# Layer 0's scans: two channel tiles at once, as two chains half a step apart

## The chip, the cores and the metric

The kernel runs on one core of a Trainium2 chip. The metric is the device time of one execution in microseconds (us). All arithmetic is in float32; the large matmuls are made of products of operands split into a rounded upper part (`whi`) and a rest (`wlo`).

## What is computed

A backbone of two layers over 256 latent tokens and a prefix of 256 context tokens, model width 2048. Each layer: a norm, a modulation by the condition, a mixer, a gated residual add. Layer 0 is a bidirectional delta-rule recurrence (32 heads of 64), layer 1 a bidirectional retention. The change concerns the recurrence of layer 0, whose step is

```
def wkv7_scan(S0, r, decay, k, v, kk, a, reverse):
    def step(S, inp):
        r_t, w_t, k_t, v_t, kk_t, a_t = inp
        sa = jnp.einsum('bhvk,bhk->bhv', S, kk_t)
        S = S * w_t[:, :, None, :] - sa[..., None] * (kk_t * a_t)[:, :, None, :] + v_t[..., None] * k_t[:, :, None, :]
        return S, jnp.einsum('bhvk,bhk->bhv', S, r_t)
...
    for d in range(2):
        S_c, oc = wkv7_scan(S0, r_c, w_c[d], k_c[d], v_c, kk_c, a_c[d], d == 1)
        _, ol = wkv7_scan(S_c, r_l, w_l[d], k_l[d], v_l, kk_l, a_l[d], d == 1)
```

## The kernel before

Channels lie in 16 tiles of 128 (two heads each); a tile is called e. Layer 0 first projects (0 to about 500 us), then works out features for every tile (to about 1015 us) and stores them in device memory (`fD`, `vcD`, and triangular blocks whose inverses come back as `Td`, `T1d`), then runs the scans (about 1018 to 1748 us), then a tail (to 1800 us) before layer 1.

The recurrence is done in chunks of 64 tokens: 8 steps for a tile, each for both directions. A step has four links, each on the result of the one before: **z** (L1322, two matmuls with the states, then a DVE add with `zv`, L1327), **u** (L1340, two matmuls with the inverted blocks `tt`, then two ACT copies, L1346), the **state products** (L1353, two matmuls, called m in the prediction), and the **state updates** (four DVE operations, L1366, or L1368 in a tile's first step). The next z needs the updates. This is "the chain".

What a step needs beforehand is made for half a tile (4 steps, a "set"; argument `hf`): `loads` brings features (`ft`, L1210 and L1213) and values (`uv`, L1219) into one of FR = 4 buffers, `tloads` brings inverses (`tt`, L1247, and `t1`, L1242), and `ahead` computes `zv` (L1263), `first` (L1277) and `second` (L1294). Behind the 4 steps come the **outs** of the set (L1399 and L1406), which use the same buffers and then free them, so that the loads of the set two further on can start. `back` finishes a tile (norm, gate; L1450 and L1460 are its transposes), and `out_chunk` multiplies finished tiles with the output weights (L1524, 512 columns a matmul) in groups of GR tiles and adds the sums to `x1` (L1533).

The order of PE, DVE, ACT and POOL is fixed by a planner, the class `Wheel`: every piece of work is given with a planned time (`W.at`), pieces are written out by planned time as soon as their buffers are free in that order, and each of these engines runs its instructions in exactly that order. A matmul that waits therefore holds everything behind it on PE. The DMA issues on SyncE (SP) are left to the scheduler, which orders them by their place in the program and by priority. PSUM has one bank each for z (`ps_p`), u with the state products (`ps_u`) and the outs (`ps_o`), three for the output chunks (`ps_b0`, `ps_b1`, `ps_t`, by `BANK`) and two for the rest (`ps_c`). `ada_line` (L350) computes parts of the condition's modulation in the tail.

The planned pace of a tile is `TE`, 40 us for the first four and 34.5 for the others.

## Time and profile before

| | us |
|---|---|
| median of 3 runs | 2850.48 |
| lowest and highest run | 2847.07 and 2854.71 |
| the profiled execution | 2847.56 |
| its span in the trace | 2845.8 |
| PE busy in the span | 2695.4 (95%) |
| mean granted TensorE clock | 0.98 |

Rows of the profile that matter here are of four kinds. A *stretch* gives the busy time of each engine between two times, the granted TensorE clock (1.00 is full speed) and the share of time in which the DMA engines were busy. A *wait* gives the engine and line that waited, what released it, the sum, the count and the longest. A *group* gathers the instructions of one line and shape: busy time, mean ns of one, and the idle time of the engine just before them. A *timeline* row has a start, a duration, the line and a count of like instructions in a row; the bracket is idle time before it. Matmuls are pipelined, so the duration of a row overlaps the next; starts tell more. PE is the matmul, PEld its weight load.

### The profile page before, as it was taken

The page shows a single profiled execution, that of the slowest core. Times are in us where ns is not written, and L with a number is a line of the kernel's source. Part 1 is how long each engine was busy: PE and PEld are TensorE (multiplying, and loading weights), DVE is VectorE, ACT ScalarE, POOL GpSimd, SP SyncE. Part 2 cuts the span into 40 slices and gives each one's busy share as a digit, 9 for nine tenths or more (in the row PEclk, how much of TensorE's full clock was granted, in tenths as well). Part 3 has the DMA queues.
Part 4 walks back from the last instruction along what each step waited for, and adds up shares of the span by engine and source line. Part 5 has one row for each costly group of instructions (what it writes and reads, how often), then busy time and mean ns, then how long its engine had stood idle before and what let it go on. Part 6 is the DMA issues. An engine that isn't in the chain of part 4 may idle for free. (4 is left out here: it accounts for less than half of the span.)

```text
span 2845.8 us, 48362 instructions
## 1 busy us (share of the span) xinstructions
PE 2695.4 (95%) x18564; PEld 2132.3 (75%) x18580; DVE 1695.0 (60%) x3142; ACT 1330.1 (47%) x2284; POOL 494.4 (17%) x368
## 2 busy tenths in 40 slices
PE   6999999999998999989888899999999999999998
PEld 4576478777776777766666676788888898899886
DVE  3565843688888754567665635875555554434444
ACT  5243732577776434444443443545444543334443
POOL 0002300000013322222212222220000079800000
PEclk9999999999999999989999999999999999999999
DMA  9778974578887766565665555565545576644654
GB/s 339 286 254 299 317 238 127 157 222 267 265 271 245 249 171 192 177 218 169 183 184 153 162 164 197 181 225 175 185 166 177 206 251 226 221 138 150 206 183 163
DMA packets 490425, 594.73 MB, mean 209 GB/s; under 512 B 122689, under 2 KB 306897, under 8 KB 487377
## 3 DMA queue, kind: packets, MB, share of 16 engines
q1 hardware_dynamic: 490194, 591.64, 64.3%
q8 instruction: 146, 2.39, 0.3%
q14 instruction: 85, 0.70, 0.1%
HBM read 464.11 MB, written 127.40 MB: 208 GB/s over the span
## 5 line engine op out<-in xcount | busy, mean ns | idle before, releaser
L394 DVE TENSOR_TENSOR wlo<-wraw,whi 128x1024 fp32r<-128x1024 f32 (+1 forms) x368 | 461.0, 1254 | 567.6 <-ACT whi L393 559.9
L393 ACT CAST whi<-wraw 128x1024 fp32r<-128x1024 f32 (+1 forms) x368 | 375.7, 1024 | 601.2 <-PE ps_acc L420 177.8
L420 PE MATMUL ps_acc<-whi,xop 128*128 128x512 f32 x1024 | 304.9, 392 | 1.3 <-DVE ev L642 0.8
L1895 PE MATMUL ps_acc<-xop,whi 128*128 128x256 f32 (+1 forms) x1024 | 255.6, 342 | 3.6 <-ACT whi L393 2.4
L420 PEld LDWEIGHTS ps_acc<-whi,xop 128*128 128x128 f32 x1024 | 192.0, 188 | 45.3 <-issue 2.9
L1895 PEld LDWEIGHTS ps_acc<-xop,whi 128*128 128x128 f32 x1024 | 178.0, 192 | 27.0 <-ACT whi L393 2.8
L1795 PEld LDWEIGHTS ps_b<-ax,xop 128*128 128x128 f32 x1536 | 190.9, 189 | 4.9 <-DVE ah L394 0.3
L1795 PE MATMUL ps_b<-ax,xop 128*128 128x256 f32 x1536 | 194.5, 283 | 0.1
L1366 DVE SCALAR_TENSOR_TENSOR s<-ps_u,ec,qs 64x64 f32<-64x64 f32 x384 | 108.6, 283 | 134.6 <-PE ps_u L1353 123.1
L420 PE MATMUL ps_acc<-wlo,xop 128*128 128x512 f32 x512 | 187.4, 393 | 0.0
L726 PE MATMUL ps_acc<-xop,whi 128*128 128x512 f32 x512 | 177.5, 406 | 2.0 <-DVE ev L642 2.0
L577 PE MATMUL ps_acc<-xop,whi 128*128 128x512 f32 x512 | 161.8, 402 | 14.8 <-ACT xop L393 13.6
L1895 PE MATMUL ps_acc<-xop,wlo 128*128 128x256 f32 (+1 forms) x512 | 172.2, 338 | 0.0
L1845 PE MATMUL ps_acc<-whi,ah 128*128 128x512 f32 x512 | 161.5, 396 | 2.1 <-DVE ah L394 2.1
L420 PE MATMUL ps_c<-whi,xop 128*128 128x512 f32 x512 | 155.3, 391 | 0.0
L1515 POOL TENSOR_TENSOR wlo<-wraw,whi 128x512 fp32r<-128x512 f32 (+2 forms) x56 | 81.7, 1458 | 363.5 <-ACT whi L1514 313.7
L1524 PE MATMUL ps_b<-yx,whi 128*128 128x512 f32 x352 | 141.0, 447 | 3.8 <-DVE x L1533 3.8
L1868 POOL TENSOR_TENSOR wga<-wga,cst 128x512 f32<-128x512 f32 x64 | 70.1, 1116 | 417.0 <-DVE xop L394 404.9
L1346 ACT ACTIVATE uv<-ps_u 64x128 f32<-64x128 f32 x256 | 69.5, 271 | 149.8 <-PE ps_u L1340 147.5
L577 PEld LDWEIGHTS ps_acc<-xop,whi 128*128 128x128 f32 x512 | 96.0, 191 | 54.0 <-ACT xop L393 17.3
L771 POOL TENSOR_TENSOR wlo<-wraw,whi 128x1024 fp32r<-128x1024 f32 x32 | 78.4, 2451 | 211.8 <-ACT whi L770 207.0
L420 PEld LDWEIGHTS ps_acc<-wlo,xop 128*128 128x128 f32 x512 | 96.7, 189 | 20.8 <-issue 0.5
(303 smaller groups left out, 5731.3 us busy)
## 6 DMA issues: line engine op xcount, KB each, us to landing
wada<-in_ada_w SPq DMA_DIRECT2D x72, 1024.0 KB, 8.5
wraw<-in_rt_w_in SPq DMA_DIRECT2D x64, 1024.0 KB, 5.2
ft<-fD SPq DMA_DIRECT2D x64, 768.0 KB, 6.5
wraw<-in_rk_w_in SPq DMA_DIRECT2D x72, 512.0 KB, 4.6
fD<-it SPq DMA_DIRECT2D x64, 512.0 KB, 4.3
wraw<-in_rt_w_in SPq DMA_DIRECT2D x64, 512.0 KB, 4.8
wraw<-in_rt_w_out SPq DMA_DIRECT2D x32, 1024.0 KB, 5.2
wraw<-in_rk_w_in SPq DMA_DIRECT2D x28, 1024.0 KB, 5.6
```

Source lines behind the costliest of these rows:

```text
L393: self.nc.scalar.copy(hi, src)
L394: (eng or self.nc.vector).tensor_tensor(lo, src, hi.bitcast(F32), ALU.subtract)
L420: nc.tensor.matmul(pt, xop(d)[:, x_, xs], ws[k // 2][w_][:, k % 2, sl], start=(d == 0 and n == 0), stop=(d == nk - 1 and n == 2))
L577: nc.tensor.matmul(acc[i], (hi, lo)[w_][:, kk, 128 * i:128 * i + 128], xs[ds[k]][:, x_, :], start=(k == 0 and n == 0), stop=(k == nk - 1 a ...
L726: nc.tensor.matmul(st["acc"][i], st["s", d // 4][w_][:, d % 4, 128 * i:128 * i + 128], self.kx[d][:, x_, :], start=(d == 0 and m == 0), st ...
L771: nc.gpsimd.tensor_tensor(st["s", c][1], st["w", c], st["s", c][0].bitcast(F32), ALU.subtract)
L1366: nc.vector.scalar_tensor_tensor(dst, src, ec, R["qs", d][H, H], ALU.mult, ALU.add)
L1515: nc.gpsimd.tensor_tensor(lo[:, 0:n, :], src, hi[:, 0:n, :].bitcast(F32), ALU.subtract)
L1524: nc.tensor.matmul(Q["p", i], Q["s", i // 2][w_][:, k, 128 * (i % 2):128 * (i % 2) + 128], st["yx", e0 + k][:, x_, :], start=(k == 0 and r ...
L1795: nc.tensor.matmul(pt[:, TL * j:TL * j + TL], ht[e][:, w_, 128 * k:128 * k + 128], ax[:, k, x_, :], start=(k == 0 and n == 0), stop=(k == ...
L1845: nc.tensor.matmul(acc[m], y[:, x_, kk, 128 * m:128 * m + 128], ws[w_][:, kk, :], start=(p == 0 and kk == 0 and n == 0), stop=(p == 7 and ...
L1895: nc.tensor.matmul(acc[i][:, 0:nt], w_[:, kk, 128 * i:128 * i + 128], x[:, x_, 0:nt], start=(d == 0 and n == 0), stop=(d == KD - 1 and n = ...
```

## The change

The tiles are taken in pairs E, E+1. Each tile of a pair is a chain of its own, and the second is half a step behind the first. Sets are quarters now (`q`, two steps of both tiles), with eight feature buffers of half the size. Each chain has one PSUM bank (`ps_p0`, `ps_p1`) in which z, u and both state products lie side by side, and each tile of a pair has a bank for its outs; the output chunks have two banks. The feature array `fD` is laid out in quarters, so its stores are runs of half the length. `back` of the odd tile comes BO = 21 us after that of the even one, the output groups are [2, 4, 4, 2, 2, 2] tiles, and the ada lines come in eight pieces of half the size. Line numbers move: `zv` is L1272, `first` L1284, `second` L1297, z L1327, u L1346, the state products L1359, the outs L1408 and L1415, the output matmuls L1540, the loads L1215, L1216 and L1221, `tt` L1253 and `t1` L1250, the transposes of `back` L1461 and L1471.

In the middle of the scans PE had, of the kernel before, the links of one chain with output matmuls between them (names: output<-moving and stationary operand):

```order
L1353 MATMUL ps_u<-uv,ft_8746 128x128
L1353 MATMUL ps_u<-uv,ft_8748 128x128
L1524 MATMUL ps_b_13420<-yx,whi 128x512
L1450 MATMUL ps_c<-c_ident,vt 128x128 x4
L1524 MATMUL ps_b_13420<-yx,whi 128x512
L1322 MATMUL ps_p<-s_8758,ft_8746 128x128
L1322 MATMUL ps_p<-s_8772,ft_8748 128x128
L1524 MATMUL ps_b_13420<-yx,wlo 128x512
L1524 MATMUL ps_b_13481<-yx,whi 128x512
L1340 MATMUL ps_u<-z,tt_8752 128x64 x2
L1524 MATMUL ps_b_13481<-yx,whi 128x512
```

and has in the changed kernel, at such a place, the links of two (`ps_p0` and `ps_p1`; the numbers tell tiles of buffers apart):

```order
L1327 MATMUL ps_p1_12948<-s101_8782,ft3_8750 128x128
L1327 MATMUL ps_p1_12948<-s111_8790,ft4_8752 128x128
L1359 MATMUL ps_p0_12883<-uv_12525,ft1_8746 128x128
L1359 MATMUL ps_p0_12883<-uv_12531,ft2_8748 128x128
L1540 MATMUL ps_b1_12946<-yx_11446,whi_12739 128x512
L1540 MATMUL ps_b1_12946<-yx_11446,wlo_12740 128x512
L1540 MATMUL ps_b1_12946<-yx_11811,whi_12739 128x512
L1346 MATMUL ps_p1_12948<-z_12951,tt0_8760 128x64 x2
L1540 MATMUL ps_b1_12946<-yx_11811,whi_12739 128x512
L1297 MATMUL ps_c_12973<-tt1_8762,x21_12943 32x32 x16
L1540 MATMUL ps_b1_12946<-yx_11811,wlo_12740 128x512
```

Between a link and the next of the same chain there now stands a link of the other chain.

SyncE's order at the first loads of a tile, before (`tt` and `t` are inverses, `ft` and `uv` features and values):

```order
L1247 DMA tt_8752<-Td 32x2x32 x2
L1242 DMA t_15207<-T1d 32x8x32
L1247 DMA tt_8752<-Td 32x2x32 x6
L1242 DMA t_15207<-T1d 32x8x32
L1247 DMA tt_8752<-Td 32x2x32 x4
L1213 DMA ft_8746<-fD 128x2x128
L1210 DMA ft_8746<-fD 128x1536
L1213 DMA ft_8746<-fD 128x2x128
L1219 DMA uv<-vcD 64x256 x2
L1210 DMA ft_8748<-fD 128x1536
L1213 DMA ft_8748<-fD 128x2x128 x2
L1219 DMA uv<-vcD 64x256 x2
```

and at the first loads of a pair in the changed kernel:

```order
L1215 DMA ft_8746<-fD 128x896
L1221 DMA uv<-vcD 64x128 x2
L1215 DMA ft_8748<-fD 128x896
L1221 DMA uv<-vcD 64x128 x2
L1253 DMA tt_8760<-Td 32x2x32 x2
L1250 DMA t_14097<-T1d 32x8x32
L1253 DMA tt_8760<-Td 32x2x32 x2
L1250 DMA t_14104<-T1d 32x8x32
L1253 DMA tt_8760<-Td 32x2x32 x2
L1250 DMA t_14104<-T1d 32x8x32
L1253 DMA tt_8760<-Td 32x2x32 x2
L1215 DMA ft_8750<-fD 128x896
```

The inverses stood ahead of all of the set's features there; now some of them stand between the features of the first tile (`ft_8746`, `ft_8748`) and those of the second (`ft_8750` and one more).

The diff, cut to its core:

```diff
-BANK = ("b0", "b1", "t")
+BANK = ("b0", "b1")
...
-GR = [2, 2, 3, 3, 3, 2, 1]
+GR = [2, 4, 4, 2, 2, 2]
...
-FR = 4
-UB, SB = 0.3, 0.58
+FR = 8
+UB, SB = 0.5, 1.05
...
+BO = 21.0
...
-        np = 2048 // n
+        nk = 2 if i else 4
+        np = 8 if i else 16
...
-        self.fD = self.dr.tile([KD, 2, 2, 128, 2048], F32, name="fD")
+        self.fD = self.dr.tile([KD, 2, 4, 128, 1024], F32, name="fD")
...
-            t = sp.tile([128, 2176], F32, name=f"ft{b}", tag=f"ft{b}")
-            nc.gpsimd.memset(t[:, 1536:].rearrange("q (m x c) -> q m x c", m=2, x=5)[:, :, 2, :], 0.0)
+            t = sp.tile([128, 1088], F32, name=f"ft{b}", tag=f"ft{b}")
+            nc.gpsimd.memset(t[:, 896:960], 0.0)
...
-            def loads(e, hf, d):
+            def loads(e, q, d):
...
-                    nc.sync.dma_start(ft[:, 0:1536], self.fD[e, d, dh, :, 0:1536])
-                    kr = self.fD[e, d, dh, :, 1536:].rearrange("q (m x c) -> q m x c", m=2, x=4)
-                    for x in (0, 2):
-                        nc.sync.dma_start(ft[:, 1536:].rearrange("q (m x c) -> q m x c", m=2, x=5)[:, :, x + x // 2:x + x // 2 + 2, :],
-                                          kr[:, :, x:x + 2, :])
+                    nc.sync.dma_start(ft[:, 0:896], self.fD[e, d, m, :, 0:896])
+                    nc.sync.dma_start(ft[:, 960:1088], self.fD[e, d, m, :, 896:])
                     st["ft"] = nc.cur_bb.bb.instructions[-1].name
-                    w = sp.tile([128, 2, 2, 128], F32, name="uv", tag="uv", bufs=FR)
+                    w = sp.tile([128, 2, 128], F32, name="uv", tag="uv", bufs=FR)
                     for p in range(2):
                         ps_ = slice(64 * p, 64 * p + 64)
-                        nc.sync.dma_start(w[ps_, p, :, :], self.vcD[e, ps_, 2 * dh:2 * dh + 2])
-                    st[e][hf, d] = {"it": ft[:, 0:1024].rearrange("q (p m h c) -> q p m h c", p=2, m=2, h=2),
-                                    "bt": ft[:, 1024:1536].rearrange("q (p m c) -> q p m c", p=2, m=2),
-                                    "kr": ft[:, 1536:2176].rearrange("q (m x c) -> q m x c", m=2, x=5),
-                                    "uv": w}
+                        nc.sync.dma_start(w[ps_, p, :], self.vcD[e, ps_, m])
...
+            def tloads(E, q):
 
                 def f():
-                    st[e]["tt", hf] = tt = self.tt[hf]
-                    for d in range(2):
-                        if hf == 0:
-                            st[e]["t1", d] = t1 = self.sp.tile([128, 8, 32], F32, name="t1", tag="t1", bufs=4)
-                        for p in range(2):
-                            hb = 64 * (1 - p)
-                            if hf == 0:
-                                nc.sync.dma_start(t1[hb:hb + 32], self.T1d[e // 2, e % 2, d, p].rearrange("u i t -> i u t"))
-                            for blk in range(2):
-                                r0 = hb + 32 * blk
-                                src = self.Td[e // 2, blk, e % 2, d, p, 4 * (1 - hf):4 * (1 - hf) + 4]
-                                for mm in range(2):
-                                    nc.sync.dma_start(tt[r0:r0 + 32, 2 * mm + p if d == 0 else 3 - 2 * mm - p, :, r0:r0 + 32],
-                                                      src[2 * mm:2 * mm + 2].rearrange("u i t -> i u t"))
+                    st[E]["tt", q] = tt = self.tt[q % 2]
+                    for e in (E, E + 1):
+                        for d in range(2):
+                            m = seq[d][2 * q] // 2
+                            if q == 0:
+                                st[e]["t1", d] = t1 = self.sp.tile([128, 8, 32], F32, name="t1", tag="t1", bufs=4)
+                            for p in range(2):
+                                hb = 64 * (1 - p)
+                                if q == 0:
+                                    nc.sync.dma_start(t1[hb:hb + 32], self.T1d[e // 2, e % 2, d, p].rearrange("u i t -> i u t"))
+                                for blk in range(2):
+                                    r0 = hb + 32 * blk
+                                    nc.sync.dma_start(tt[r0:r0 + 32, slot(e, d, p), :, r0:r0 + 32],
+                                                      self.Td[e // 2, blk, e % 2, d, p, 2 * m:2 * m + 2].rearrange("u i t -> i u t"))
...
                     P["z"] = self.psum("c")
+                    for e in (E, E + 1):
+                        for s in range(2 * q, 2 * q + 2):
+                            for h in range(2):
+                                for d in range(2):
+                                    _, p, B, V = where(d, s)
+                                    S = st[e][q, d]
+                                    o = 128 * (2 * (e % 2) + s % 2) + 64 * h
+                                    nc.tensor.matmul(P["z"][B, o:o + 64], S["it"][V, p, h, B], S["uv"][V, p, 64 * h:64 * h + 64],
+                                                     start=True, stop=True)
...
-                hf, k = s // 4, s % 4
+                E, ch, q = e - e % 2, e % 2, s // 2
+                k = 2 * ch + s % 2
                 R = {}
+                state = lambda d, s: self.S[ch, d, s % 4]
+
+                def bank():
+                    R["p"] = self.psum(f"p{ch}")
 
                 def z():
...
-                    R["p"] = self.psum("p")
+                    bank()
                     for d in range(2):
-                        _, _, mm, p, _, _ = w[d]
-                        nc.tensor.matmul(R["p"][:, 0:128], st[e][hf, d]["kr"][:, mm, 2 - p:4 - p, :].rearrange("q x c -> q (x c)"),
-                                         self.S[d, s], start=(d == 0), stop=(d == 1))
+                        p = w[d][1]
+                        nc.tensor.matmul(R["p"][:, 0:128], st[e][q, d]["kr"][:, 2 - p:4 - p, :].rearrange("q x c -> q (x c)"),
+                                         state(d, s), start=(d == 0), stop=(d == 1))
...
-                    R["u"] = self.psum("u")
-                    rhs = R["z"] if s else st[e]["zv", hf][:, 0, :]
+                    assert st[E][q, "ready"]
+                    if not s:
+                        bank()
+                    rhs = R["z"] if s else st[E]["zv", 0][:, k, :]
                     for h in range(2):
-                        nc.tensor.matmul(R["u"][:, 64 * h:64 * h + 64], st[e]["tt", hf][:, k, h, :],
+                        nc.tensor.matmul(R["p"][:, 128 + 64 * h:192 + 64 * h], st[E]["tt", q][:, k, h, :],
...
-                J, jz, ju = "chain", ("zp", e, s), ("zu", e, s)
+                J, r, key = ("chain", ch), ("p", ch), ("p", e, s)
+                nd = ((r, 1, key),)
                 if s:
-                    W.at(t, z, J, (("zp", 1, jz),))
-                    W.at(t + 0.01, zc, J, (), (jz,))
+                    W.at(t, z, J, nd)
+                    W.at(t + 0.01, zc, J)
                     if s < 7:
                         for d in range(2):
                             W.at(t + 0.02, qs(d), J)
-                W.at(t + UB * Ts, u, J, (("zu", 1, ju),))
+                W.at(t + UB * Ts, u, J, () if s else nd)
                 for d in range(2):
-                    W.at(t + UB * Ts + 0.01, uc(d), J, (), (ju,) if s == 7 and d else ())
+                    W.at(t + UB * Ts + 0.01, uc(d), J, (), (key,) if s == 7 and d else ())
                 if s < 7:
                     for d in range(2):
                         W.at(t + SB * Ts, sm(d), J)
                     for d in range(2):
-                        W.at(t + SB * Ts + 0.01, sc(d), J, (), (ju,) if d else ())
-
-            def outs(e, hf):
+                        W.at(t + SB * Ts + 0.01, sc(d), J, (), (key,) if d else ())
...
+                    for e in (E, E + 1):
+                        if q == 0:
+                            st[e]["o"] = self.psum(f"o{e % 2}")
...
+                if e % 2 and not q:
+                    W.at(t0, oc, (e - 1, "o"), (), (("o", e),))
+                    t0 += BO
...
-                            Q["p", i] = self.psum(BANK[(4 * eg + i) % 3])
+                            Q["p", i] = self.psum(BANK[i % 2])
...
+            for E in range(0, KD, 2):
+                Ts = (te[E + 2] - te[E]) / 16
+                for q in range(4):
+                    h0 = te[E] + 4 * Ts * q
+                    for x, (e, d) in enumerate(((E, 0), (E, 1), (E + 1, 0), (E + 1, 1))):
+                        W.at((h0 - LD + 0.85 * x if E or q else tl + 1.5 + x), loads(e, q, d), "fl", (("f", FR, (e, q, d)),))
+                    W.at(h0 - 3.5 * Ts if E or q else tl + 1.5, tloads(E, q))
+                    zv, zvc, first, cp1, second, cp2 = ahead(E, q)
+                    j = (E, "i", q)
                     W.at(h0 - 1.3 * Ts, zv, (j, "z"), (("c", 2, (j, "z")),))
                     W.at(h0 - 1.3 * Ts + 0.02, zvc, (j, "z"), (), ((j, "z"),))
                     W.at(h0 - 1.3 * Ts + 0.01, first, j, (("c", 2, (j, 0)),))
                     W.at(h0 - 1.3 * Ts + 0.9, cp1, j, (), ((j, 0),))
                     W.at(h0 - 0.3 * Ts, second, j, (("c", 2, (j, 1)),))
                     W.at(h0 - 0.3 * Ts + 0.7, cp2, j, (), ((j, 1),))
-                    for s in range(4 * hf, 4 * hf + 4):
-                        step(e, s, t + s * Ts, Ts)
-                    W.at(h0 + 4 * Ts + 0.08 * (Tn if hf else Ts), outs(e, hf), (e, "o"), (("o", 1, ("o", e)),) if hf == 0 else (),
-                         tuple((e, hf, d) for d in range(2)))
-                back(e, te[e + 1] + 0.3 + 0.1 * Tn)
+                    for s in range(2 * q, 2 * q + 2):
+                        for e in (E, E + 1):
+                            step(e, s, te[E] + (2 * s + e % 2) * Ts, Ts)
+                    W.at(h0 + 4.2 * Ts, outs(E, q), (E, "o"), tuple((("o", e % 2), 1, ("o", e)) for e in (E, E + 1)) if q == 0 else (),
+                         tuple((e, q, d) for e in (E, E + 1) for d in range(2)))
+                for e in (E, E + 1):
+                    self.tb[e] = te[E + 2] + 0.3 * Ts + (1.5 if e == KD - 1 else 0.01 * (e % 2))
+                    back(e, self.tb[e])
...
+            done = lambda e: self.tb[e] + (9 if e >= KD - TB else 16 + BO * (e % 2))
             t0, t1 = tx + 9, te[KD] + BK
-            av = [max(t0 + (t1 - t0) * e0 / 15, te[e0 + n] + (BK if e0 + n > KD - TB else 16.5)) for e0, n in groups]
-            av.append(av[-1] + 13)
+            av = [max(t0 + (t1 - t0) * e0 / 15, done(e0 + n - 1)) for e0, n in groups]
+            av.append(av[-1] + 24)
```

More of the change, by code (lines that the diff above doesn't have):

```diff
@@ L346, in f @@
                 if x == 0:
-                    st["p"] = self.psum("o" if i else "t")
-                kq, c = x % 4, n * (x // 4)
-                for g in range(4):
-                    nc.tensor.matmul(st["p"][32 * g:32 * g + 32, c:c + n], self.cstat(kq * 4 + g), st[x][:, g, :],
-                                     start=(kq == 0), stop=(kq == 3))
+                    st["p"] = self.psum("o0" if i else "t")
+                k0, c = x * nk % 16, n * (x * nk // 16)
+                for g in range(nk):
+                    k = k0 + g
+                    nc.tensor.matmul(st["p"][32 * (k % 4):32 * (k % 4) + 32, c:c + n], self.cstat(k), st[x][:, g, :],
+                                     start=(k < 4), stop=(k >= 12))
             return f
@@ L1155, in open_scans @@
             self.tt.append(t)
-        for d in range(2):
-            for k in range(1, 8):
-                s = sp.tile([128, 128], F32, name=f"s{d}{k}", tag=f"s{d}{k}")
-                nc.gpsimd.memset(s, 0.0)
-                self.S[d, k] = s
+        for c in range(2):
+            for d in range(2):
+                for k in range(4):
+                    s = sp.tile([128, 128], F32, name=f"s{c}{d}{k}", tag=f"s{c}{d}{k}")
+                    nc.gpsimd.memset(s, 0.0)
+                    self.S[c, d, k] = s
     def next_ft(self):
@@ new lines, in f @@
+                    for e in (E, E + 1):
+                        if q == 0:
+                            st[e]["o"] = self.psum(f"o{e % 2}")
+                            nc.tensor.matmul(st[e]["o"], self.zer[:, 0:128], self.zer, start=True, stop=False)
+                    for e in (E, E + 1):
+                        o = st[e]["o"]
+                        for s in range(2 * q, 2 * q + 2):
+                            w = [where(d, s) for d in range(2)]
+                            if s:
+                                for d in range(2):
+                                    c, p, _, V = w[d]
+                                    nc.tensor.matmul(o[V, 128 * (c // 2):128 * (c // 2) + 128], st[e][q, d]["kr"][:, 4 * p, :],
+                                                     self.S[e % 2, d, s % 4], start=False, stop=False)
+                            for h in range(2):
+                                for d in range(2):
+                                    c, p, _, V = w[d]
+                                    o0 = 128 * (c // 2) + 64 * h
+                                    S = st[e][q, d]
+                                    nc.tensor.matmul(o[V, o0:o0 + 64], S["it"][:, p, h, V], S["uv"][:, p, 64 * h:64 * h + 64],
+                                                     start=False, stop=(s == 7 and h == 1))
@@ L1485, in back @@
                 for k, f in zip(tl_, (vm, trv, bv, oc, sq, red, sqr, rec, om, tro, comb, gm, spl)):
-                    W.at(t0 + k, f, (e, "v" if q and f in (vm, trv, bv) else "o"),
-                         (("c", 2, (e, f)),) if f in (trv, tro) else (("y", 6, ("y", e)),) if f is spl and t0 + 14 >= tx else (),
+                    if f is oc and e % 2 and not q:
+                        continue
+                    W.at(t0 + k, f, (e - e % 2, "o") if f is oc else (e, "v") if q and f in (vm, trv, bv) else "back",
+                         (("c", 2, (e, f)),) if f in (trv, tro) else (("y", 7, ("y", e)),) if f is spl and t0 + 14 >= tx else (),
                          {oc: (("o", e),), bv: ((e, trv),), comb: ((e, tro),)}.get(f, ()))
@@ L1568, in out_chunk @@
                     if e0 + n == KD:
-                        W.at(te + 2, fin(i), "fin", (("y", 6, (eg, i)),))
+                        W.at(te + 2, fin(i), "fin", (("y", 7, (eg, i)),))
                         W.at(te + 4, nrm(i), "fin", (), ((eg, i),))
-            for e in range(KD):
-                t = te[e]
-                Ts = (te[e + 1] - t) / 8
-                Tn = (te[e + 2] - te[e + 1]) / 8 if e < KD - 1 else 0
-                for hf in range(2):
-                    h0 = t + 4 * Ts * hf
-                    for d in range(2):
-                        W.at((h0 - LD + 1.7 * d if e or hf else tl + 1.5 + d), loads(e, hf, d), "fl", (("f", FR, (e, hf, d)),))
-                    W.at(h0 - 3.5 * Ts if e or hf else tl + 1.5, tloads(e, hf))
-                    zv, zvc, first, cp1, second, cp2 = ahead(e, hf)
-                    j = (e, "i", hf)
+            for E in range(0, KD, 2):
[7 more added lines that the diff above has]
+                    j = (E, "i", q)
                     W.at(h0 - 1.3 * Ts, zv, (j, "z"), (("c", 2, (j, "z")),))
```

149 lines of the change are left out of this document (63 added, 86 removed).

## The prediction

> **What bounds the kernel now.** I read the busy time by stretch first, because the page's shares are averages over stages. The columns after the stretch and its length are busy time and instruction count of PE, PEld, DVE, ACT and POOL, then the granted clock, the DMA share and GB/s.
>
> ```profile
> 1015.00:1200.00 185.00, 174.74 (x1731) 140.66 (x1736) 95.91 (x266) 82.54 (x201) 44.82 (x24) 0.95 0.63 181
> 1200.00:1400.00 200.00, 173.29 (x1938) 130.56 (x1940) 129.55 (x378) 84.12 (x230) 44.45 (x36) 0.95 0.61 188
> 1400.00:1600.00 200.00, 173.98 (x1934) 129.12 (x1939) 127.24 (x366) 81.89 (x225) 39.85 (x28) 0.97 0.57 171
> 1600.00:1750.00 150.00, 138.94 (x1433) 108.03 (x1437) 76.90 (x218) 62.16 (x166) 36.97 (x26) 0.98 0.52 156
> 1750.00:1800.00 50.00, 44.57 (x253) 22.52 (x250) 27.97 (x63) 17.71 (x34) 13.54 (x14) 0.95 0.73 247
> ```
>
> The scans run from 1018 to 1748 us. PE is idle there for 10.3 + 26.7 + 26.0 + 11.1 = 74 us, more than anywhere else in the program, and a granted clock of 0.95 means that a tenth of the stretch ran at half clock: 18.5 + 20 + 12 + 6 = 56 us in all. PE is busy or waiting in order, so two questions follow: what does it wait for, and what would be late next? The view of waits over the scans (engine, line, releaser, us, times, longest) answers the first; the view of line groups (us busy, mean ns, then idle before) gives the price of one weight load and the idle time at the features.
>
> ```profile
> PEld ps_u L1340 <- DVE z L1327: 47.2, 68, 5.9
> PEld ps_u L1353 <- ACT uv L1346: 46.5, 96, 0.9
> PEld ps_p L1322 <- DVE s L1366: 25.8, 72, 0.8
> PE ps_u L1340 <- DVE z L1327: 20.9, 25, 5.7
> PEld ps_p L1322 <- DVE s L1368: 11.2, 28, 0.9
> L1340 PEld LDWEIGHTS ps_u<-z,tt 128*128 128x128 f32 x448 | 64.5, 197 | 51.2 <-DVE z L1327 47.2
> L1263 PE MATMUL ps_c<-uv,ft 64*64 64x64 f32 x992 | 43.9, 236 | 15.4 <-DMA uv<-vcD 14.1 <-DMA tt<-Td 1.1
> L1263 PEld LDWEIGHTS ps_c<-uv,ft 64*64 64x64 f32 x992 | 38.0, 147 | 23.6 <-issue 17.0 <-DMA uv<-vcD 2.9 <-PE ps_u L1353 1.7
> ```
>
> The five chain rows add up to 151.6 us. 264 of these waits are the weight loader's, and while it waits the matmuls ahead still run for about one load, 197 ns: 264 x 0.197 = 52 us that PE didn't lose. So **the chain's own latency costs PE about 100 us**. The features' first product (L1263) waits for its loads: 15.4 us of PE idle for certain, and with the weight loader's idle time, part of which PE still worked through, at most 15.4 + 23.6 = 39; I take 25. By this reading the chain is the limit and the loads are almost hidden. The timeline shows how nearly they are not (start, us, count, idle before):
>
> ```profile
> 1550.26 0.40 PE L1406 MATMUL ps_o<-uv,ft 128*64 128x64 f32 x8
> 1550.93 0.55 PE L1340 MATMUL ps_u<-z,tt 128*128 128x64 f32 x4
> 1555.23 0.66 PE L1340 MATMUL ps_u<-z,tt 128*128 128x64 f32 x4
> 1559.55 0.66 PE L1340 MATMUL ps_u<-z,tt 128*128 128x64 f32 x4
> 1561.50 0.33 PE L1263 MATMUL ps_c<-uv,ft 64*64 64x64 f32 x2
> 1562.96 1.94 PE L1263 MATMUL ps_c<-uv,ft 64*64 64x64 f32 x30 [1.14 <-DMA tt<-Td]
> ```
>
> A set of loads can only start when the outs (L1406) of the set two back have freed its buffers. The outs end at 1550.66; the last load lets L1263 go on at 1562.96, **12.3 us later**. Between them the chain made two and a half steps of 4.30 us, most of it stall. The chain's stalls and the loads' round trip lie side by side, and nearly of the same length. SyncE's timeline has the round trip's parts:
>
> ```profile
> 1550.96 1.42 SPq L1213 DMA_DIRECT2D ft<-fD  x1
> 1552.47 0.41 SPq L1210 DMA_DIRECT2D ft<-fD  x1
> 1553.45 1.09 SPq L1219 DMA_DIRECT2D uv<-vcD  x2
> 1556.26 2.33 SPq L1219 DMA_DIRECT2D uv<-vcD  x2
> 1286.73 0.92 SPq L1247 DMA_DIRECT2D tt<-Td  x2
> ```
>
> 0.3 us after the outs the first issue, then ten issues of about 0.5 us with some slow ones up to 1558.6, then some 4 us until the last one has landed.
>
> **The change, part by part.** My sum is made against the profiled execution's 2847.56 us (span 2845.8); the median shown is 2850.48, so 2.9 us are added at the end.
>
> *Two chains.* A stalled step is 4.30 us (1550.93 to 1555.23). Its work at full rate is less; the unstalled end of the scans has the prices:
>
> ```profile
> 1743.86 0.60 PE L1353 MATMUL ps_u<-uv,ft 128*128 128x128 f32 x4
> 1744.22 0.48 PE L1524 MATMUL ps_t<-yx,wlo 128*128 128x512 f32 x1
> 1744.54 0.40 PE L1524 MATMUL ps_b<-yx,whi 128*128 128x512 f32 x1
> 1744.77 0.60 PE L1450 MATMUL ps_c<-c_ident,vt 128*128 128x128 f32 x4
> ```
>
> A chain group takes 0.36 us, the first 512-column matmul behind it 0.32, each further one 0.23. A step of three groups and six such matmuls is 3 x 0.36 + 3 x 0.32 + 3 x 0.23 = 2.7 us, so 1.6 us of 4.3 is latency. With the chains half a step apart, two steps and their side work, 5.4 us, stand in the loop of 4.3 us: it is covered. A few waits stay, where a features block or outs stand askew; one shared bank per chain also makes the next z wait for all four state updates. I leave 20 us of 100: **-80** (ends -100 and -55).
>
> *Loads.* Nothing in the change shortens the round trip: eight buffers of half the size hold the same two sets, a set has the same bytes, and its loads become 16 issues where they were ten. At 0.5 us an issue the last goes out 8 us after the first, against 7.6 in the set above, with the same landing behind it. I take 11.5 us from the end of the outs to the last load (ends 9 and 13). What changes is how much work lies in that time. From the new order, at the prices above, there are 6.6 us of PE work between the outs of a set and the features that need its buffers, plus 0.8 us of crossings and waits: 7.4. In 17 sets from the third pair on L1272 then holds PE for 11.5 - 7.4 = 4.1 us: 70 us. The early sets have over 10 us there and hardly wait. In six sets, the first of a pair, SyncE's order puts 7 to 15 loads of inverses between the features of the first tile and those of the second; the tt row above gives 0.46 us each, so these sets land about 4.5 us later, and some have more work to cover it: 6 x 7 = 42 us. Together 112 against today's 25: **+87** (ends +10 and +115). Every instruction of both chains is queued behind the waiting L1272, so this wait is not filled by the other chain.
>
> *The clock.* The same view of stretches, cut at one wait, and the same two products in a set without it:
>
> ```profile
> 1478.00:1494.60 16.60, 12.99 (x108) 9.30 (x107) 14.05 (x35) 6.76 (x19) 4.91 (x3) 1.00 0.68 203
> 1494.60:1501.40 6.80, 5.83 (x72) 5.17 (x72) 0.99 (x4) 2.01 (x5) 1.36 (x1) 0.50 0.21 49
> 1494.88 1.94 PE L1263 MATMUL ps_c<-uv,ft 64*64 64x64 f32 x30 [2.74 <-DMA uv<-vcD]
> 1497.51 1.07 PE L1277 MATMUL ps_c<-t,ft 32*32 32x32 f32 x32 [0.69 <-ACT zv L1268]
> 1472.51 1.14 PE L1263 MATMUL ps_c<-uv,ft 64*64 64x64 f32 x30 [1.06 <-DMA uv<-vcD]
> 1473.58 0.69 PE L1277 MATMUL ps_c<-t,ft 32*32 32x32 f32 x32
> ```
>
> A wait of 2.74 us is followed by 6.8 us at half clock, in which work of 1.14 and 0.69 us takes 1.94 and 1.07: about 0.4 of the 5.83 busy us is lost, 2.3 us. One of 1.06 us leaves the clock alone, though the 1.14 us at 1562.96 did not. Today's 56 us at half clock cost about a third, 19 us. With 23 waits over 2 us at 2 us each it becomes 46: **+27** (ends 0 and +45).
>
> The Trainium skill, "TensorE: Matmul & The Clock Gate", section "HAM oscillation", sets the bound at idle gaps above about 3.4 us; here 2.74 us was enough, so the trace decides against it. By that bound only the six long waits would count, and the term would be about +5.
>
> *Side work.* Waits of the feature products behind their copies (L1277 above, 0.69 us, is one) fall inside longer waits: **-8** (ends -15, 0). Out-projection matmuls behind the last chain step go from 83 to 128 in the order: 45 x 0.23 = 10 us leave the scans and come back in the tail, where two banks instead of three make each chunk of six matmuls wait for its adds; the tail's squares and sums overlap better in return. The row 1750 to 1800 has only 5.4 us of idle to hide anything: **0** (ends -6, +16). The ada loads in half-size pieces fill the same tail; they are in those ends.
>
> *Stores of the features* in runs half as long. The stage has spare PE cover but a busy DMA:
>
> ```profile
> 700.00:900.00 200.00, 188.75 (x1311) 143.72 (x1310) 175.77 (x274) 146.57 (x220) 27.15 (x18) 0.97 0.84 260
> fD<-it SPq DMA_DIRECT2D x64, 512.0 KB, 4.3
> ```
>
> The bytes are the same; what hides more packets is DMA time of 0.16 of the stretch. **+2** (ends 0, +8).
>
> The sum: -80 + 87 + 27 - 8 + 0 + 2 = **+28** us, 2875.6 on the profiled execution. The half clock and the waits overlap somewhat (a window that begins inside a wait costs nothing until the wait ends), so I take 3 off: 2872.5 there, **2875 us** against the median.
>
> **Rivals.** (1) *The loads land sooner*, and the change pays. Half-size buffers are freed tile by tile, so the first two could start nearly 1 us before the outs are all done, and DMA was on average only 0.6 busy. If the round trip were 9 us, ordinary sets would wait 17 x 1.6 = 27 us, the term of the loads would be 27 + 42 - 25 = +44, and the clock's about +8: -80 + 44 + 8 - 8 + 2 = -34, or 2816 us. Without the delay of the six first sets it is 2786. It decides from a round trip of about 10.2 us downward. Against it: 12.3 us measured, and more issues per set. (2) *The clock holds.* It falls only in the six long waits, 7 us each, and stays up over those of 4 us, as it did over 1.06 us. Six waits with some 4 us lost behind each are 24 against today's 19, +5 instead of +27: -80 + 87 + 5 - 8 + 2 = +6, 2853.6 profiled, or 2856 against the median: no change. It decides from a half clock after fewer than about half of the 17 ordinary waits. Against it: the window behind 2.74 us, and the one behind 1.14 us. By the bound of the Trainium skill named above it would fall out so. (3) *The tail* gives back more than it saves: at its upper end of +16 us the forecast becomes 2891; this lies inside my forecast's own range. (4) *The chains are not really apart.* The stalls would stay and nothing would change. The new order shows z, u and m of the two banks alternating, so this gets no more than 0.01, counted with (2).
>
> **How the numbers follow.** Forecast (loads take the place of the chain's waits, and PE's clock falls) 0.49, own range 2859 to 2905; the clock holds 0.17; loads sooner 0.34. What a measurement here can tell from no change is about 0.3%, 8.5 us: above 2859 is slower, below 2842 faster. So slower 0.49, same 0.17, faster 0.34. Low end: rival 1 runs from 2786 to 2840; 2800 leaves out less than a tenth. High end: a round trip of 13 us adds 17 x 1.5 = 26 us and gives 2901; 2905 leaves out as much.
>
> **What would show it.** In the new trace, chain waits of u, m and z should fall from 152 us in those rows to under 50; L1272 should idle over 80 us with DMA as the releaser; the granted clock in the scans should fall below 0.93; the tail from the last outs to the first matmul of layer 1 should be near 58 us instead of the 48.1 between these rows.
>
> ```profile
> 1751.29 0.40 PE L1406 MATMUL ps_o<-uv,ft 128*64 128x64 f32 x8
> 1799.77 1.65 PE L1895 MATMUL ps_acc<-xop,whi 128*128 128x256 f32 x4 [1.11 <-ACT xop L1646]
> ```
>
> If L1272 waits less than 50 us, the term of the loads was wrong and the kernel is faster. If the chain rows stay above 80 us, the first term was wrong.

## The result, and the profile after

The changed kernel takes 2901.21 us (median; 2898.28 to 2907.31) against 2852.6 us of the kernel before, measured beside it: a ratio of 1.0175 with an interval of 1.0152 to 1.0199. It is slower by some 49 us where 25 were forecast; the range was exceeded on no side (it ended at 2905), but the size was missed by a factor of two. The profiled execution's span is 2905.2 us, 59.4 more than before.

Three marks place the 59.4 us: the first u of the scans, the last outs, and the first matmul of layer 1. They stood at 1020.36, 1751.69 and 1799.77 us and stand here (timeline of the changed kernel):

```profile
1027.62 0.55 PE L1346 MATMUL ps_p<-zv,tt 128*128 128x64 f32 x4
1793.68 0.40 PE L1415 MATMUL ps_o<-uv,ft 128*64 128x64 f32 x8
1859.47 1.65 PE L1913 MATMUL ps_acc<-xop,whi 128*128 128x256 f32 x4 [1.11 <-ACT xop L1664]
```

The scans begin 7.3 us later, last 766.5 us and not 731.3 (+35.1), and the tail is 65.4 us long and not 48.1 (+17.3). The view by stretch and the line groups (us busy, mean ns, then idle before) show what the scans spend it on:

```profile
1015.00:1200.00 185.00, 165.43 (x1664) 138.94 (x1666) 92.99 (x247) 73.80 (x186) 41.10 (x21) 0.90 0.62 181
1200.00:1400.00 200.00, 156.30 (x1788) 130.41 (x1790) 119.70 (x323) 74.20 (x214) 35.40 (x27) 0.82 0.59 173
1400.00:1600.00 200.00, 161.69 (x1800) 133.45 (x1801) 127.66 (x335) 73.36 (x205) 39.04 (x24) 0.90 0.55 161
1600.00:1795.00 195.00, 168.36 (x1863) 139.73 (x1867) 109.87 (x287) 77.70 (x215) 47.89 (x36) 0.93 0.53 154
L1272 PE MATMUL ps_c<-uv,ft 64*64 64x64 f32 x1006 | 54.8, 247 | 93.2 <-DMA uv<-vcD 92.9
L1327 PE MATMUL ps_p<-s,ft 128*128 128x128 f32 x448 | 78.6, 304 | 4.5 <-DVE s L1374 4.4
L1359 PE MATMUL ps_p<-uv,ft 128*128 128x128 f32 x448 | 75.1, 294 | 0.8 <-ACT uv L1352 0.7
L1346 PE MATMUL ps_p<-z,tt 128*128 128x64 f32 x448 | 68.2, 277 | 28.6 <-DVE z L1332 28.4
```

The idle time at the feature products went from 15.4 to 93.2 us, with a load as the releaser. The granted clock says that 18.5 + 36 + 20 + 13.7 = 88 us worth of clock was lost, so 176 us ran at half clock where 56 did (21 windows in the trace, and seven before). The links m and z of the chains hardly wait any more; u still does (waits, 1015 to 1795 us):

```profile
PEld ps_p L1346 <- DVE z L1332: 36.7, 28, 2.9
PE ps_p L1346 <- DVE z L1332: 28.4, 27, 2.6
```

The first set of a pair shows the path of the loads (PE, then rows picked from SyncE's in the same stretch):

```profile
1398.02 0.40 PE L1415 MATMUL ps_o<-uv,ft 128*64 128x64 f32 x8
1406.06 1.10 PE L1272 MATMUL ps_c<-uv,ft 64*64 64x64 f32 x16
1415.99 0.44 PE L1272 MATMUL ps_c<-uv,ft 64*64 64x64 f32 x2 [8.82 <-DMA uv<-vcD]
1417.76 1.11 PE L1272 MATMUL ps_c<-uv,ft 64*64 64x64 f32 x14 [1.32 <-DMA uv<-vcD]
...
1398.76 1.87 SPq L1215 DMA_DIRECT2D ft<-fD  x1
1400.72 1.09 SPq L1221 DMA_DIRECT2D uv<-vcD  x2
1403.67 0.58 SPq L1250 DMA_DIRECT2D t<-T1d  x1
1410.03 0.92 SPq L1253 DMA_DIRECT2D tt<-Td  x2
1411.04 0.37 SPq L1215 DMA_DIRECT2D ft<-fD  x1
1414.28 1.09 SPq L1221 DMA_DIRECT2D uv<-vcD  x2
```

SyncE issues almost without a break from the outs to the last value load, 17 us, with twelve loads of inverses in between, and the last load releases L1272 19.3 us after the outs.

### The profile page after: what moved, and what is told of

It reads as the page before. It is cut to its first block, busy times and chain, and to the rows that moved or that the text cites. A ratio compares the mean times of both kernels' runs of the same rounds, so it can differ in the third digit from the quotient of the medians.

```text
span 2905.2 us, 48870 instructions
## 1 busy us (share of the span) xinstructions
PE 2697.7 (93%) x18572; PEld 2168.1 (75%) x18580; DVE 1720.6 (59%) x3110; ACT 1318.0 (45%) x2274; POOL 493.7 (17%) x366
## 4 chain that ended last, share of the span: by engine, by line
PE 71%; DMA 9%; DVE 6%; SPq 4%; POOL 3%; ACT 3%; issue 3%; DVEq 0%; ACTq 0%; POOLq 0%
PE ps_acc L423 12%; PE ps_acc L1913 9%; PE ps_acc L580 6%; PE ps_c L423 5%; PE ps_acc L729 5%; PE ps_b L1540 5%; PE ps_b L1813 4%; PE ps_acc L1863 4%; DMA uv<-vcD 3%; PE ps_b L783 3%; PE ps_acc L783 2%; PE ps_b L314 2%; PE ps_b L1002 2%; DMA wga<-in_ada_w 2%; POOL wga L1886 2%
## 5 line engine op out<-in xcount | busy, mean ns | idle before, releaser
L1540 PE MATMUL ps_b<-yx,whi 128*128 128x512 f32 x512 | 221.0, 457 | 5.0 <-DVE x L1549 3.3
L1352 ACT ACTIVATE uv<-ps_p 64x128 f32<-64x128 f32 x256 | 69.6, 272 | 287.0 <-PE ps_p L1346 274.6
L580 PE MATMUL ps_acc<-xop,whi 128*128 128x512 f32 x512 | 162.5, 403 | 14.3 <-ACT xop L396 13.7
L1332 DVE TENSOR_TENSOR z<-ps_p,zv 128x128 f32<-128x128 f32 x112 | 32.4, 289 | 236.1 <-PE ps_p L1327 223.6
L1531 POOL TENSOR_TENSOR wlo<-wraw,whi 128x512 fp32r<-128x512 f32 (+1 forms) x48 | 80.8, 1684 | 403.7 <-ACT whi L1530 353.1
L1272 PE MATMUL ps_c<-uv,ft 64*64 64x64 f32 x1024 | 55.6, 246 | 93.2 <-DMA uv<-vcD 92.9
L580 PEld LDWEIGHTS ps_acc<-xop,whi 128*128 128x128 f32 x512 | 96.6, 192 | 53.7 <-ACT xop L396 17.3
L1372 DVE SCALAR_TENSOR_TENSOR s<-ps_p,ec,qs 64x64 f32<-64x64 f32 x384 | 108.6, 283 | 32.0 <-PE ps_p L1359 24.9
```

The costliest lines, as they stand in the source:

```text
L580: nc.tensor.matmul(acc[i], (hi, lo)[w_][:, kk, 128 * i:128 * i + 128], xs[ds[k]][:, x_, :], start=(k == 0 and n == 0), stop=(k == nk - 1 a ...
L1372: nc.vector.scalar_tensor_tensor(dst, src, ec, R["qs", d][H, H], ALU.mult, ALU.add)
L1540: nc.tensor.matmul(Q["p", i], Q["s", i // 2][w_][:, k, 128 * (i % 2):128 * (i % 2) + 128], st["yx", e0 + k][:, x_, :], start=(k == 0 and r ...
```

## The experiments

All ratios are to the kernel before on the same chip. Where the median of the kernel before is needed it was 2850 to 2852 us in these jobs. The theory at the start was the prediction's: the loads' round trip behind the outs holds L1272, and the clock falls behind each wait.

**No loads of features and values**, in either kernel: they are left out behind the first two sets of the changed kernel and behind the first tile of the kernel before, and later sets use what lies in the buffers, so the results are not those of the scans. The edit of the changed kernel begins so, and the other is like it (line numbers differ by a few where an edit adds or removes lines).

```diff
-                    nc.sync.dma_start(ft[:, 0:896], self.fD[e, d, m, :, 0:896])
+                    if e < 2 and q < 2:
+                        nc.sync.dma_start(ft[:, 0:896], self.fD[e, d, m, :, 0:896])
...
```

> The changed kernel, with feature and value loads only for the first two sets; later sets use what lies in the buffers, so the scans' values are wrong and 240 loads of features and 240 of values are left out. Theory (loads hold L1272, and PE's clock falls behind those waits): the waits of L1272 go, about 95 us from the third set on, with some 40 us of the half clock; the time falls by 90 to 140 us, to 2760 to 2810. Rival (the chains' own latency, z to u above all, sets the pace and would fill the gap again): falls by less than 30 us.

> The kernel before, with feature and value loads only for the first tile; later tiles use what lies in the buffers, so the scans' values are wrong and the loads of 30 half sets are left out. Theory: the chain's latency remains and takes the place of the loads: falls by 15 to 40 us, to 2810 to 2835. Rival (the loads already set the pace of the kernel before): falls by 60 us or more. The difference to the first run of this job says what the two chains are worth where no load holds them: theory 30 to 60 us in their favour, less the tail.

2783.27 us (ratio 0.9766, 0.9751 to 0.978) and 2817.68 us (0.9881, 0.9864 to 0.9897). These loads, with the half clock that follows their waits, cost the changed kernel 118 us and the kernel before 33: +85, and without them the two chains are ahead by 34. So the result parts into two: 85 - 34 = 51. In the traces the scans take 646.5 against 700.7 us without loads, so the chains' own gain is 54 us, of which the longer tail takes back 16 and a later start 2.

**Filling a wait.** 16 zero matmuls ahead of L1272 in seven first sets.

```diff
+                    if E and q == 0:
+                        for _ in range(16):
+                            nc.tensor.matmul(P["z"], self.zer[:, 0:128], self.zer, start=True, stop=True)
```

> The changed kernel, with 16 matmuls of zeros (about 3.5 us) ahead of L1272 in the first set of each pair from the second pair on, where it waits 4 to 11 us for loads. They compute nothing that is used. Theory (the idle wait costs the clock as well): the waits stay, the half-clock windows behind these seven sets go, 10 to 25 us less in all. Rival (the half clock is only a mark of a wait and costs little): no change, or up to 10 us more.

2908.95 us (1.0204, 1.0177 to 1.023): a miss, with a median 8 us above the changed kernel's, though the two intervals overlap. The mean clock went from 0.961 to 0.963 only. The idle time at the feature products fell by 27 us to 65.9, about what the fill itself takes (25.4): it stood in the waits and shortened nothing. How much the clock costs on its own stays open; the run shows that it isn't got back so cheaply.

**The order on SyncE, and a later L1272.**

```diff
-                    W.at(h0 - 3.5 * Ts if E or q else tl + 1.5, tloads(E, q))
+                    W.at(h0 - LD - 0.5 if E or q else tl + 1.5, tloads(E, q))
```

> The changed kernel, with the inverses' loads of every set planned 1.9 us ahead of its features' loads (they were planned 1.4 us behind them), so that on SyncE they no longer stand between the features of the two tiles. Theory (the delay of the first sets is SyncE's order): the waits in the first sets of the seven later pairs fall from some 50 us to 20, with part of the clock behind them: 25 to 55 us less, 2846 to 2876. Rival (these sets wait for bandwidth, not for the order): within 8 us of the changed kernel.

```diff
-                    W.at(h0 - 1.3 * Ts, zv, (j, "z"), (("c", 2, (j, "z")),))
+                    W.at(h0 - 0.9 * Ts, zv, (j, "z"), (("c", 2, (j, "z")),))
...
-                    W.at(h0 - 0.3 * Ts, second, j, (("c", 2, (j, 1)),))
+                    W.at(h0 - 0.1 * Ts, second, j, (("c", 2, (j, 1)),))
```

> The changed kernel, with the feature products planned 0.4 of a step (1.7 us) later and the second ones 0.2 of a step later, so that more work lies between the outs and L1272. Theory (the wait at L1272 is the round trip less the work in it): each of some 28 waits falls by 1 to 2 us, and short ones leave the clock alone: 30 to 60 us less, 2840 to 2870. Rival (the chains only wait elsewhere, at u behind the later features): within 10 us of 2901.

2900.52 us (1.0176, 1.0161 to 1.0191) and 2898.25 us (1.0159, 1.014 to 1.0179): neither moves. Both are misses of the theory. With all the inverses ahead, the outs of the same set ended at 1398.5 us and its features and values went out from 1404.0 to 1412.9, because SyncE was still issuing inverses when the buffers came free; the last went out 14 us behind the outs where it had been 17, and L1272's idle time fell only to 89.5 us. With L1272 later, its idle time was 81.0 us and not 93.2. If a fixed time behind the outs held the loads, more work in it should have hidden them. What both runs leave as it was is SyncE's work in a set. That is the second theory: **the number of SyncE's issues sets when the loads land**, 32 of loads in a set and 40 in a first one, at about half a us each, in sets of 24 us (766.5 / 32) that have other transfers as well.

**Number of issues.** Without the inverses' loads in the changed kernel (behind the first pair, later pairs use the inverses that lie in the buffers), and with more issues of the same bytes in the kernel before:

```diff
+                    if E:
...
+                        return
```

> The changed kernel, with loads of inverses (tt and t1) only for the first pair; later pairs use what lies in the buffers, so the scans' values are wrong and 16 to 24 small loads are left out of each set. Feature loads are as they were. Theory (the loads are late because SyncE, at 0.46 us an issue, has 32 to 40 of them to send in a set of 22 us): the waits at L1272 fall by half or more, 2901 falls by 40 to 90 us, most of it in the first sets of the pairs. Rival (the loads are late because they can only start behind the outs and then need their 10 us): falls by less than 25 us.

```diff
-                    nc.sync.dma_start(ft[:, 0:1536], self.fD[e, d, dh, :, 0:1536])
+                    for x in (0, 768):
+                        nc.sync.dma_start(ft[:, x:x + 768], self.fD[e, d, dh, :, x:x + 768])
...
-                        nc.sync.dma_start(w[ps_, p, :, :], self.vcD[e, ps_, 2 * dh:2 * dh + 2])
+                        for m in range(2):
+                            nc.sync.dma_start(w[ps_, p, m, :], self.vcD[e, ps_, 2 * dh + m])
```

> The kernel before, with each set's ten feature and value loads cut into 16 of the same bytes. Nothing else differs. Theory (the number of issues lengthens the round trip, and the kernel before hides it only just): 10 to 40 us more, 2860 to 2890. Rival (the round trip is bytes and latency, the number of issues is hidden): within 8 us of 2850.

2828.4 us (0.9916, 0.9894 to 0.9938): 73 less than the changed kernel, though the loads left out move only 8 KB each (32 KB for t1). And 2908.87 us (1.0198, 1.0182 to 1.0213): **six more issues in each set cost the one chain 57 us**, as much as the whole change. That is more than the 10 to 40 us expected. The cut also makes the runs of a transfer shorter: 154832 DMA packets moved from 1015 to 1750 us where 143414 did, so this run alone does not part issues from packets. The changed kernel has no more packets than the kernel before, 142101.

SyncE's own waits fit the theory, but only as a sum. Three rows of the kernel before, three of the changed kernel and one of the run without inverses (waits of the queue, 1015 to 1750 us):

```profile
SPq L1247 <- DMA ft<-fD: 44.2, 46, 3.2
SPq L1213 <- PE ps_o L1399: 17.8, 11, 2.8
SPq L1213 <- PE ps_o L1406: 3.6, 13, 0.4
```

```profile
SPq L1253 <- PE ps_p L1346: 30.9, 20, 4.2
SPq L1216 <- PE ps_o L1408: 13.1, 14, 2.3
SPq L1216 <- PE ps_o L1415: 10.5, 21, 2.1
```

```profile
SPq L1216 <- PE ps_o L1413: 143.2, 22, 12.3
```

For the outs, SyncE waits 21.4 us in the kernel before and 23.6 in the changed one, which does not tell the two apart. All of its waits together are 244.6 us in the kernel before, 145.1 in the changed kernel and 155.1 in the kernel before with 16 issues. So SyncE has less slack in the two slow kernels, but it is not full: the 1125 issues of the changed kernel hold it for 554 of the 735 us, and its longest row is a wait of the inverses' loads for u, the last to read the buffers that they fill. It is late where it counts, in the stretch behind the outs shown above. Without the inverses it comes early and waits 143.2 us for the outs. The kernel before has some room: 44.2 us in which its small loads waited for earlier loads, of which the changed kernel has 5.0. In the kernel before with 16 issues the feature products wait as in the changed kernel:

```profile
L1265 PE MATMUL ps_c<-uv,ft 64*64 64x64 f32 x992 | 51.2, 254 | 52.7 <-DMA uv<-vcD 48.5 <-DMA tt<-Td 4.2
```

**The tail.** Output groups with a last one of two, in the kernel before:

```diff
-GR = [2, 2, 3, 3, 3, 2, 1]
+GR = [2, 3, 3, 3, 3, 2]
...
-            av.append(av[-1] + 13)
+            av.append(av[-1] + 24)
```

> The kernel before with output groups [2, 3, 3, 3, 3, 2] and the last group's time of the change; 118 instead of 74 output matmuls stand behind the last outs. Theory (moved work alone is paid in the tail and given back in the scans only where PE has no holes): the tail grows by 8 to 12 us, the scans give back less than 5, so 5 to 12 us more in all. Rival (the tail of the change is long because of its two banks): within 4 us of 2850.

2856.42 us (1.0017, 1.0003 to 1.003). In its trace the tail is 58.3 us, 10.2 longer, and the scans take 732.0 us, no shorter: there the moved work is paid in full. The medians differ by only 5 us (1 to 9 by the interval), so part of it may be given back. It accounts for up to 10 of the 17 us; the rest (half-size ada pieces, two banks) was not taken apart.

**Fewer issues, with the two chains.** One load brings both tiles' inverses (16 to 8 a set, for three more stores of inverses a pair); then also one load of values for two:

```diff
-                self.Td = self.dr.tile([8, 2, 2, 2, 2, 8, 32, 32], F32, name="Td")
+                self.Td = self.dr.tile([8, 2, 2, 2, 4, 2, 2, 32, 32], F32, name="Td")
...
+                                    nc.sync.dma_start(tt[r0:r0 + 32, x:x + 2, :, r0:r0 + 32].rearrange("i e u t -> i (e u) t"),
+                                                      self.Td[E // 2, blk, d, p, m].rearrange("e u i t -> i (e u) t"))
```

> The changed kernel with the inverses laid out so that one load brings the blocks of both tiles of a pair: 8 loads of tt a set instead of 16, the same bytes (and four stores of inverses a pair instead of one). Theory (SyncE's issues, not bytes or the round trip, hold the loads; six more issues a set cost the kernel before 57 us): 35 to 60 us less than 2901, 2840 to 2866. Rival (it is the waiting of the small loads on PE that holds the queue, not their number): less than 15 us.

```diff
-                    for p in range(2):
-                        ps_ = slice(64 * p, 64 * p + 64)
-                        nc.sync.dma_start(w[ps_, p, :], self.vcD[e, ps_, m])
+                    nc.sync.dma_start(w, self.vcD[e, :, m].unsqueeze(1).broadcast_to([128, 2, 128]))
```

> As the run with half the loads of tt, and each pair of 32 KB value loads is one load of 128 KB that writes both halves of the buffer (the half not needed is overwritten by u): 12 issues of features and values a set instead of 16, 256 KB more. Theory: another 12 to 35 us less, 2810 to 2850, which beats the kernel before if it goes below 2842. Rival (with fewer issues the bytes hold, and there are more of them): no gain over the run before it.

2858.28 us (1.0034, 1.0015 to 1.0054), 43 less than the changed kernel, and **2827.01 us (0.9926, 0.9901 to 0.9951)**, 74 less and faster than both kernels, with 256 KB more to move in each set. Issues are the price, not bytes, and not packets either: from 1015 to 1750 us the first of the two runs moves 142563 packets and the second 158332, the most of these kernels. Nor is it the small loads' waiting on PE that holds the queue, the rival of the first run: that wait grew from 30.9 to 86.2 us there (99.5 in the second), while the time fell. SyncE's waits add up to 252.1 and 344.5 us. The feature products wait 35.8 us in the second run:

```profile
L1272 PE MATMUL ps_c<-uv,ft 64*64 64x64 f32 x992 | 48.3, 238 | 35.8 <-DMA uv<-vcD 35.7
```

**Another engine as issuer.** The inverses' loads from ACT, planned 0.9 of a step later:

```diff
-                                    nc.sync.dma_start(tt[r0:r0 + 32, slot(e, d, p), :, r0:r0 + 32],
+                                    nc.scalar.dma_start(tt[r0:r0 + 32, slot(e, d, p), :, r0:r0 + 32],
...
-                    W.at(h0 - 3.5 * Ts if E or q else tl + 1.5, tloads(E, q))
+                    W.at(h0 - 2.6 * Ts if E or q else tl + 1.5, tloads(E, q))
```

> The changed kernel with the 16 loads of tt of a set issued from ScalarE, 0.9 of a step later than before so that their buffer is free, and not from SyncE; number and bytes as they were. Theory (it is SyncE's time): the waits at L1272 fall as without loads of inverses, 73 us there, less what 16 issues of ACT cost the chains: 20 to 65 us less than 2901. Rival (the DMA engines or the landing hold the loads, whichever engine issues): within 15 us, or slower by what ACT loses.

3087.29 us (1.0839, 1.0815 to 1.0863): a miss. A new wait took the place of the old one: ACT runs in its fixed order, and the copies that the chains need (L1352) stood behind issues that waited (in the stretch from 1188 to 1202 us for earlier loads to land). L1272 no longer appears among PE's long waits (waits from 1015 to 1950 us).

```profile
PE ps_p L1359 <- ACT uv L1352: 272.8, 31, 17.3
ACT uv L1352 <- DMA tt<-Td: 261.6, 22, 18.1
```

**Fewer issues, with one chain**, to be fair to the kernel before:

```diff
-                    for p in range(2):
-                        ps_ = slice(64 * p, 64 * p + 64)
-                        nc.sync.dma_start(w[ps_, p, :, :], self.vcD[e, ps_, 2 * dh:2 * dh + 2])
+                    nc.sync.dma_start(w, self.vcD[e, :, 2 * dh:2 * dh + 2].unsqueeze(1).broadcast_to([128, 2, 2, 128]))
```

> The kernel before with each pair of 64 KB value loads as one load of 256 KB that writes both halves of the buffer (the half not needed is overwritten by u): 8 issues of features and values a set instead of ten, 256 KB more. Theory (its loads are hidden but for some 25 us, and the chain's latency is next): 0 to 15 us less than 2850, so that two chains with fewer issues (2827) stay ahead of one chain with fewer issues by 10 us or more. Rival (fewer issues help the one chain as much as the two): below 2833.

2848.95 us (0.9984, 0.9967 to 1.0001): no change, though 256 KB more are moved in each set here as well. With two chains each saving of issues paid. That with one chain the chain's latency is next in line would explain the difference; no run shows it.

## Why the prediction was half right

The way it went was the likeliest case's: most of the chain's waits went, the loads' waits and the half clock took their place, and the marks named ahead mostly came out (idle at L1272 over 80 us: 93.2; the clock below 0.93 in three of four stretches; a longer tail; chain rows down from 152 us, though to some 70 and not below 50).

The size did not. The 25 us forecast and the 49 measured are both what is left of larger terms. The forecast had -80 for the chains, 87 + 27 - 8 - 3 = +103 for the loads, the clock and what falls inside them, +2 for the stores and 0 for the tail. The runs with and without loads give -54 in the scans, +85 for the loads with the clock, +16 for the tail and +2 at the start. So loads and clock together were put too high, by 18 us, and **the terms that failed in size are the chains' (-80, measured -54) and the tail's (0, measured +16)**. **The step that failed in its mechanism is the loads'**: a round trip behind the outs, where the runs show the number of SyncE's issues. That errors of 26, 18 and 16 us left the result inside the range is in part luck. Step by step:

- *Two chains, -80.* Mis-sized, for two reasons that the traces show. The 100 us count a wait twice: PE's row of 20.9 us lies inside the weight loader's waits (of the 30.1 us that PE idles at the three links in the kernel before, 30.0 fall into waits of the loader), so the same reckoning with the loader's rows alone, 130.7 - 52, gives 79. And the loop was called covered, with 20 us left: m and z are covered, z to u is not. PE idles 28.6 us at L1346, more than the 21.7 at L1340 before, and without loads the weight loader waits 37.9 us for z in the changed kernel against 46.6 in the kernel before. DVE does the inverses' work in between, in its fixed order, and one such instruction can be long (last section); that it makes up the whole of these waits is not shown.
- *Loads, +87.* The size was near: the idle time at the features grew by 78 us. The mechanism was not "nothing in the change shortens the round trip", with 11.5 us from the outs to the last load and 16 issues at 0.5 us counted as hidden within it. There the queue was treated as free when the outs end. It isn't: with the inverses' loads, SyncE is still issuing then, 17 us long in the set shown. The ten issues that became 16 and the inverses between the features, reckoned as a latency and a delay, are one cause, issues on one queue. Moving the inverses or L1272 in time gained nothing; taking issues away gained 43 and 74 us.
- *The clock, +27.* Too small if it goes by time at half clock: 176 us and not 56, and at the third that the forecast took for the loss +40. The count was right: PE idles for more than 2 us 23 times in these scans (19 times at L1272, three at u, once at z). The windows at half clock were longer than the 6 us that 2 us of loss stand for, 8.4 us on average. But 78 and 40 are more than the 85 that leaving out the loads gives, so the two overlap, and what the clock costs alone stays open.
- *Side work, -8 and 0.* The idle time behind the copies went from 6.3 us (L1277) to 1.4 (L1284), most of the -8. The 0 failed: the tail's +17 stands, and no trace shows the scans giving something back for the 45 matmuls that left them.
- *The first set.* Not in the sum: the scans begin 7.3 us later in this trace (2 to 5 in those of its variants), since the first pair's last values stand behind 16 loads of inverses.
- *Stores, +2.* Too small to be seen: the first features product runs at 1008.4 and not at 1006.6 us, and at 1004.5 to 1007.0 in five variants with the same stores.

Rival 1 (loads sooner) had 2816 us; where the loads do come sooner the kernel takes 2827, but fewer issues bring that about, not smaller buffers, so the nearness of the two numbers is luck. Rival 2 (the clock holds) is refuted: there are 21 windows at half clock, where it had them behind six waits only.

## What to carry to other kernels

When loads are cut into smaller ones, count the issues of the queue in one period of the loop, all of them, and compare with the period, before any latency is reckoned. No engine shows such a queue as busy; add up all of its waits rather than read one row (145.1 us in the changed kernel, 344.5 in its fastest variant with all loads), and look at what it does between the moment when buffers come free and the last load that needs them. Work moved off a path with holes lengthens the place where it arrives (here by 10.2 us), and the path itself need not get shorter. And count a wait once: where two engines wait for the same thing, the two rows overlap.

## What the runs showed of the hardware

- The price of an issue: six more in a set, of the same bytes, cost 57 us over the scans' 32 sets, 0.3 us for each, some two thirds of the 0.49 us for which one holds SyncE on average in that run.
- A DVE instruction that takes 0.41 us took 2.46 us beside a POOL instruction of 2.54 us, and ended 0.27 us after it (DVE, then POOL, changed kernel). The u behind it found PE idle for 1.55 us. It is no single case: of the 418 instructions of these two lines (L1107 and L1114) in the scans 50 took more than 0.7 us, and each of the 50 ended 0.05 to 0.27 us after the end of a POOL instruction that ran beside it; of the shorter 368, 34 ran beside one.

```profile
1537.88 0.41 DVE L1107 TENSOR_TENSOR invT<-invX 128x240 f32<-128x240 f32 x1
1540.54 2.46 DVE L1107 TENSOR_TENSOR invT<-invX 128x238 f32<-128x238 f32 x1
1540.19 2.54 POOL L1531 TENSOR_TENSOR wlo<-wraw,whi 128x1024 fp32r<-128x1024 f32 x1
1544.51 0.63 PE L1346 MATMUL ps_p<-z,tt 128*128 128x64 f32 x4 [1.55 <-DVE z L1332]
```
